# Taking TensorE's closing wait out of a kernel for a batch of expert layers

## The chip, the core and the metric

The kernel runs on one core of one Trainium2 chip. A core has five engines, each with its own list of instructions: TensorE (PE in the profile, with the loading of weights shown apart as PEld), VectorE (DVE), ScalarE (ACT), GpSimd (POOL) and SyncE (SP). The engines order themselves by semaphores: an instruction can raise one, and another can wait until it has reached a value. Transfers between the chip's memory and the core's own memory (DMAs) are issued by SP and POOL here, run by themselves, and raise a semaphore by 16 when they have landed.

The metric is the time of one execution on the device, in microseconds (us). The profile shows a span: from the first instruction of the program to the end of its last one. The time is a little longer than the span.

## The reference

Eight experts, each a two-layer network with a ReLU between the layers, applied to 256 rows of its own:

```python
# x: (8, 256, 512), w1: (8, 512, 2048), w2: (8, 2048, 512), float32
def reference(x, w1, w2):
    h = np.matmul(x, w1)
    h = np.maximum(h, 0)
    return np.matmul(h, w2).astype(np.float32)
```

## The kernel before

All work is in bfloat16 with sums in float32. The list of every engine is written by hand, and each engine runs its own in order; nothing is rearranged by a scheduler. What orders the engines against each other are the semaphores alone.

**Loads.** SP issues the first half of x (`x_f`, line 90). POOL issues the second half (`x_c`, line 140) and all the weights: for each expert one transfer of w1 (line 130) and one of w2 (line 135; the last w2 in two, lines 137 and 138). The weights have room for two experts, so that POOL waits before each later load until PE has used what lay there.

**Computation.** ACT and DVE put x into bfloat16 (line 175), PE turns it round by 64 transposes (line 243), and ACT and DVE copy the result to `xe` (lines 191 and 194). Then PE runs a loop over pairs of experts. For each of the two it computes the first layer (line 259), ACT and DVE apply the ReLU (lines 207 and 224), and then, again for each of the two, PE computes the second layer into `pt_o` (line 281). The last two matmuls of each second layer raise `s_o`, by which ACT (line 211, and for the last two experts line 214) and DVE (line 228, last two experts alone) copy `pt_o` to `out_sb`.

**Stores.** `out_sb` goes out in three transfers, each with its own semaphore of the list `s_out`:

- `s_out[0]`: experts 0 to 3, 2048 KB, issued by POOL (line 164);
- `s_out[1]`: experts 4 to 6, 1536 KB, issued by SP (line 124) when expert 6 is copied;
- `s_out[2]`: expert 7, 512 KB, issued by SP (line 126) when expert 7 is copied.

**The end.** The lists of ACT, DVE and POOL end with their last copy or store (POOL's with a drain of its own work). The function ends with these lines, which belong to two engines:

```python
    pe.wait_ge(s_out[1], 16)

    for s in s_out:
        sp.wait_ge(s, 16)
```

The first is line 290, the last instruction of PE's list. The other is line 293: SP waits for all three stores. As built, SP has two waiting instructions there, one for `s_out[1]`, and after it one for `s_out[2]` and `s_out[0]` together.

Of the kernel before, what the change touches and what calls it, by code (L numbers as in the profile page):

```python
# [9 lines left out]
def kernel(  # L10
# [55 lines left out]
    s_out = [sem(f"s_out{i}") for i in range(3)]  # L66
# [15 lines left out]
    sp, pool, act, dve, pe = nc.sync, nc.gpsimd, nc.scalar, nc.vector, nc.tensor  # L82
# [163 lines left out]
    with pe.Fori(0, G) as g:  # L246
# [21 lines left out]
        with pe.Fori(0, 2) as b:  # L268
            for kt in range(KT2):
# [10 lines left out]
                for m in range(MT):  # L280
# [6 lines left out]
                    )  # L287
                    if kt == KT2 - 1:
                        ins.then_inc(s_o, 1)
    pe.wait_ge(s_out[1], 16)  # L290

    for s in s_out:
        sp.wait_ge(s, 16)
# [30 lines left out]
```

## Time and profile before

| what | value |
|---|---|
| time, median of 3 runs | 181.29 us (181.14 to 182.26) |
| time of the profiled execution | 180.94 us |
| its span | 179.2 us |
| PE busy | 128.7 us, 72% |
| PEld busy | 88.3 us, 49% |
| ACT busy | 54.1 us, 30% |
| DVE busy | 40.9 us, 23% |
| POOL busy | 13.8 us, 8% |
| share of the 16 DMA engines' time taken by the software queue (POOL's) | 93.7% |
| the same by the hardware queue (SP's) | 6.0% |
| mean granted TensorE clock | 0.989 |

An engine's busy time counts its computing instructions. Waits on semaphores, branches and the issuing of transfers are not in it. The profile can still list a wait as an instruction of the line that made it: an entry `PEldq` or `SPq` is such an instruction of PE's or SP's queue, and its duration is that of the instruction once its condition holds, not the time spent waiting. For a transfer the profile gives the time from its issue to its landing.

### The profile page before, as it was taken

Reading aid. Unit: us, or ns where it says so; the run is one execution under the profiler, and the core shown is the slowest. Engines: PE = TensorE matmul, PEld = TensorE weight load, DVE = VectorE, ACT = ScalarE, POOL = GpSimd, SP = SyncE. Lnnn points to the kernel's source line nnn. Section 1 sums busy time; section 2 is a strip of 40 time slices with the busy share of each in tenths; the row PEclk is TensorE's granted clock in tenths of the full one; section 3 lists DMA queues with packets and bytes.
Section 4 is the critical chain, followed back from the end, with each engine's and each line's share of the span. In section 5 each row is a group of like instructions: output and inputs, shape, how many; then the busy total and the mean of one; then the engine's idle time right before and its main releaser. Section 6 shows DMA issues by size and latency. Waiting matters only on the chain. (4 is left out here: it accounts for less than half of the span.)

```text
span 179.2 us, 2548 instructions
## 1 busy us (share of the span) xinstructions
PE 128.7 (72%) x824; PEld 88.3 (49%) x832; DVE 40.9 (23%) x42; ACT 54.1 (30%) x49; POOL 13.8 (8%) x25
## 2 busy tenths in 40 slices
PE   0040403099799979979997998989589596989890
PEld 0030303078687434868742487874134485854330
DVE  0725527262333000333300033330000132310100
ACT  2759596952222020422202033130200231220100
POOL 3910000000101010110101010000100400000000
PEclk9999999999999999999999999999969999999999
DMA  5999999989989999999998999999999899999997
GB/s 192 340 225 234 212 198 234 227 187 230 227 187 230 227 198 219 234 216 194 234 223 190 230 227 198 219 234 216 194 234 223 190 230 227 198 210 216 305 420 302
DMA packets 4240, 40.90 MB, mean 228 GB/s; under 512 B 400, under 2 KB 400, under 8 KB 2064
## 3 DMA queue, kind: packets, MB, share of 16 engines
q0 software_dynamic: 3120, 36.70, 93.7%
q1 hardware_dynamic: 1120, 4.19, 6.0%
HBM read 71.30 MB, written 4.19 MB: 421 GB/s over the span
## 5 line engine op out<-in xcount | busy, mean ns | idle before, releaser
L259 PE MATMUL pt_h<-xe,w_sb 128*128 x512 | 64.0, 280 | 7.8 <-PEq L85 6.9
L259 PEld LDWEIGHTS pt_h<-xe,w_sb 128*128 x512 | 56.9, 146 | 15.3 <-issue 14.1
L281 PE MATMUL pt_o<-w_sb,ht_sb 128*128 x248 | 57.8, 387 | 7.7 <-PEq L85 6.1
L224 DVE TENSOR_SCALAR ht_sb<-pt_h 128x512 bf16<-128x512 f32 x32 | 22.1, 692 | 97.0 <-PE pt_h L259 97.0
L281 PEld LDWEIGHTS pt_o<-w_sb,ht_sb 128*128 x256 | 24.9, 99 | 39.4 <-issue 13.1
L207 ACT ACTIVATE ht_sb<-pt_h 128x512 bf16<-128x512 f32 x32 | 19.1, 597 | 49.1 <-PE pt_h L259 49.1
L243 PE MATMUL pt_tr<-identity,x_b 128*128 128x128 bf16 x64 | 7.5, 309 | 30.2 <-PEq L85 30.2
L243 PEld LDWEIGHTS pt_tr<-identity,x_b 128*128 128x128 bf16 x64 | 6.5, 142 | 30.9 <-issue 30.9
L211 ACT COPY out_sb<-pt_o 128x1024 f32<-128x1024 f32 x6 | 6.1, 1017 | 44.7 <-PE pt_o L281 44.7
L175 ACT CAST x_b<-x_f 128x1024 bf16<-128x1024 f32 x2 | 10.3, 5174 | 1.5 <-DMA x_f<-in_x_dram 1.5
L130 POOL DMA_DIRECT2D w_sb<-in_w_dram x8 | 4.2, 533 | 77.7 <-PE pt_h L259 77.7
L175 ACT COPY x_b<-x_c 128x1024 bf16<-128x1024 bf16 x2 | 9.6, 4778 | 0.0
L135 POOL DMA_DIRECT2D w_sb<-in_w_dram x7 | 6.4, 913 | 35.6 <-PE pt_o L281 35.5
L175 DVE CAST x_b<-x_f 128x1024 bf16<-128x1024 f32 x2 | 6.1, 3058 | 5.6 <-DMA x_f<-in_x_dram 5.6
L194 DVE COPY xe<-pt_tr 128x1024 bf16<-128x1024 bf16 x2 | 4.9, 2460 | 8.5 <-PE pt_tr L243 8.5
L194 ACT COPY xe<-pt_tr 128x1024 bf16<-128x1024 bf16 x2 | 5.0, 2483 | 4.1 <-PE pt_tr L243 4.1
L214 ACT COPY out_sb<-pt_o 128x512 f32<-128x512 f32 x2 | 1.2, 585 | 14.6 <-PE pt_o L281 14.6
L175 DVE COPY x_b<-x_c 128x1024 bf16<-128x1024 bf16 x2 | 5.4, 2680 | 0.0
L228 DVE COPY out_sb<-pt_o 128x512 f32<-128x512 f32 x2 | 1.4, 692 | 15.0 <-PE pt_o L281 15.0
L191 ACT COPY xe<-pt_tr 128x1024 bf16<-128x1024 bf16 x2 | 2.0, 1012 | 4.1 <-PE pt_tr L243 4.1
L191 DVE COPY xe<-pt_tr 128x1024 bf16<-128x1024 bf16 x2 | 1.4, 691 | 7.8 <-PE pt_tr L243 7.8
L175 ACT ACT_TABLE_LOAD x1 | 1.3, 1283 | 2.9 <-PEq L96 2.9
(10 smaller groups left out, 3.4 us busy)
## 6 DMA issues: line engine op xcount, KB each, us to landing
w_sb<-in_w_dram POOLq DMA_DIRECT2D x15, 2048.0 KB, 24.9
x_f<-in_x_dram SPq DMA_DIRECT2D x4, 512.0 KB, 4.6
out_dram<-out_sb POOLq DMA_DIRECT2D x1, 2048.0 KB, 34.5
out_dram<-out_sb SPq DMA_DIRECT2D x1, 1536.0 KB, 8.6
w_sb<-in_w_dram POOLq DMA_DIRECT2D x1, 1152.0 KB, 25.3
x_c<-in_x_dram POOLq DMA_DIRECT2D x1, 1024.0 KB, 10.7
w_sb<-in_w_dram POOLq DMA_DIRECT2D x1, 896.0 KB, 29.0
out_dram<-out_sb SPq DMA_DIRECT2D x1, 512.0 KB, 4.0
```

The lines of the kernel that those rows point to most:

```text
L130: pool.dma_start(w1_k[:, e % 2 * KT1:(e % 2 + 1) * KT1], w1_r[e]).then_inc(s_w1[e], 16)
L135: pool.dma_start(w2_k[:, k:k + KT2], w2_r[e]).then_inc(s_w2[e], 16)
L175: copy(x_b[:, b].rearrange("p (t m) q -> p m q t", m=MT), src.rearrange("p m (q t) -> p m q t", t=KT1),).then_inc(t_xb, 1)
L191: copy(xe[:, a * n:(a + 1) * n], pt[b][:].rearrange("p j q -> p (j q)")).then_inc(s_xe[b], 1)
L194: copy(xl[:, :, :, :, a - G].rearrange("p l j q -> p j l q"), pt[b][:].rearrange("p j (l q) -> p j l q", l=G),).then_inc(s_xe[b], 1)
L207: act.activation(ht[:, k:k + FB // 2, :C], ph[1][:], relu).then_inc(t_ha, 1)
L211: act.copy(o_sb[:, e + b], po[:]).then_inc(s_act, 1)
L224: dve.tensor_relu(ht[:, k:k + FB // 2, :C], ph[0][:]).then_inc(t_hb, 1)
L228: dve.tensor_copy(o_sb[:, e + b, 0], po[:, 0]).then_inc(s_dve, 1)
L243: ins = pe.transpose(pt[b][:, j], x_b[:, b, j], identity[:])
L259: ins = pe.matmul(ph[i // 2][:, i % 2, :], ws[i % 2 * KT1 + kt], xs[kt], start=(kt == 0), stop=(kt == KT1 - 1),)
L281: ins = pe.matmul(po[:, m], hs[(kt - k0) * MT + m], ws[kt - k0], start=(kt == 0), stop=(kt == KT2 - 1),)
```

## The change

The wait at the end of PE's list is deleted. PE's list then ends with the loop over pairs of experts, as ACT's and DVE's end with their last copies. The waits of SP stay.

```diff
@@ -287,7 +287,6 @@
                     )
                     if kt == KT2 - 1:
                         ins.then_inc(s_o, 1)
-    pe.wait_ge(s_out[1], 16)
 
     for s in s_out:
         sp.wait_ge(s, 16)
```

The built programs differ in that one instruction: every other instruction stands on the same engine, in the same order, with the same waits.

## The prediction

> **What bounds the kernel now.** I read the views from the outside in: first the page for the span, then the window table over the last part, then the order of instructions there, and last the waits that end the program. The page's stores and the clock come first.
>
> ```profile
> span 179.2 us, 2548 instructions
> PEclk9999999999999999999999999999969999999999
> DMA  5999999989989999999998999999999899999997
> out_dram<-out_sb POOLq DMA_DIRECT2D x1, 2048.0 KB, 34.5
> out_dram<-out_sb SPq DMA_DIRECT2D x1, 1536.0 KB, 8.6
> out_dram<-out_sb SPq DMA_DIRECT2D x1, 512.0 KB, 4.0
> ```
>
> The row DMA is near 9 in almost every one of the 40 slices: through its body the kernel is bound by transfers. The change touches nothing in that body, so what it is worth has to be read at the very end. There, three stores remain, and the last column says how long each takes from its issue to its landing. The timeline of the end, in order of start, says when the work before them is over (columns: start, duration, engine, line, what, and the idle time before):
>
> ```profile
> 167.37 7.07 PE L281 MATMUL pt_o<-w_sb,ht_sb 128*128 x31 [0.79 <-PEq L85]
> 169.25 0.40 SPq L124 DMA_DIRECT2D out_dram<-out_sb  x1
> 174.26 0.69 DVE L228 COPY out_sb<-pt_o 128x512 f32<-128x512 f32 x1 [7.17 <-PE pt_o L281]
> 174.47 0.58 ACT L214 COPY out_sb<-pt_o 128x512 f32<-128x512 f32 x1 [7.27 <-PE pt_o L281]
> 175.09 0.35 SPq L126 DMA_DIRECT2D out_dram<-out_sb  x1
> ```
>
> The matmuls end at 167.37 + 7.07 = 174.44 us. ACT's copy ends at 174.47 + 0.58 = 175.05, and SP issues the last store at 175.09. From there no engine computes any more. The stores land, by these starts and the times to landing above, at 169.25 + 8.6 = 177.85 (`s_out[1]`) and at 175.09 + 4.0 = 179.09 (`s_out[2]`). POOL's store, `s_out[0]`, needs one row more, that of its line:
>
> ```profile
> L164 POOL DMA_DIRECT2D out_dram<-out_sb x1: 763/763/763, 140.6 to 140.6; - x1
> ```
>
> 140.6 + 34.5 = 175.1. So the three land in the order `s_out[0]`, `s_out[1]`, `s_out[2]`, with about 1.2 us between the last two. Then the waits themselves, PE's at line 290 and SP's at line 293 (duration least/median/most in ns, then the first and last start), and SP's time spent waiting there (total, times, longest):
>
> ```profile
> L290 PEldq EVENT_SEMAPHORE  x1: 51/51/51, 177.9 to 177.9; - x1
> L293 SPq EVENT_SEMAPHORE  x2: 17/22/28, 177.9 to 179.2; - x2
> SPq L293 <- DMA out_dram<-out_sb: 3.7, 2, 2.4
> ```
>
> PE's wait and SP's first one pass together at 177.9, when `s_out[1]` lands. SP's second passes at 179.2, where the span ends. Of SP's 3.7 us there, 2.4 go to the first wait and 3.7 - 2.4 = 1.3 to the second. **What ends the program is SP's wait for the last store; PE's wait is over 1.3 us earlier.**
>
> **The change part by part.** There is one part: PE's wait goes. It removes one instruction of 51 ns, which passes at 177.9. What it moves is the moment at which PE has nothing left in its list: from 177.9 + 0.05 = 177.95 to the end of its matmuls, 174.44, which is 3.5 us earlier. It adds nothing, and no transfer, loop or load is moved past another: the lists are otherwise the same.
>
> Three questions decide the sum. *Who waits for PE?* Behind the removed instruction PE has nothing queued in this program, and nobody else waits for what PE would do after its matmuls; the last thing that others take from PE is `pt_o`, at 174.26 and 174.47 in the timeline. So inside the span the gain is 0. *What is late next?* The wait was never the latest; SP's second wait at 179.2 stays, and it depends on a store issued at 175.09, which depends on ACT and DVE, not on PE's ending. *What lies outside the span?* The profiled execution took 180.94 us, so 180.94 - 179.2 = 1.74 us lie around the span, in which the core closes the execution; no view shows who does what in it. This is the only place where an earlier PE could count.
>
> I bound that unknown from both sides. On the one side, all 1.74 us could be PE's own closing work, begun only when its list is done: then it would now begin 3.5 us earlier, and the end could fall at most to SP's 179.2, a gain of 1.74 us. On the other side, PE's closing could cost something where it now lies. A meeting of the engines is shown at the start of the program, and two rows of the waits give its price to the engine that comes early:
>
> ```profile
> SPq L308 <- PEq L308: 0.7, 1, 0.7
> POOL x_c L140 <- POOLq L96: 2.9, 1, 2.9
> ```
>
> In the first, SP waits 0.7 us for PE until all engines have met; the second is the 2.9 us that POOL spends on all that stands ahead of its first transfer, SP's first loads and several meetings among it. I take 0.7 as the price of one meeting more and keep 2.9 as the far end, which would need a whole opening to be repeated. What value do I take? By the first of these rows the one who comes early waits and the last to come lets all go. If the close has such a meeting too, the last to come is SP at 179.2, before the change and after it, and PE only waits longer. The value is therefore 0, from the row nearest to the situation; the range keeps a part of both ends.
>
> [...]
>
> A second price concerns the clock of TensorE. The window table shows it where PE has finished (columns: window, length, busy time and count of PE, PEld, DVE, ACT, POOL, granted clock, share of the DMA engines, GB/s):
>
> ```profile
> 174.45:177.90 3.45, 0.00 (x0) 0.00 (x0) 0.50 (x1) 0.58 (x1) 0.00 (x0) 1.00 1.00 412
> 177.90:179.20 1.30, 0.00 (x0) 0.00 (x0) 0.00 (x0) 0.00 (x0) 0.00 (x0) 0.86 0.06 22
> ```
>
> PE computes nothing in either window. The granted clock is 1.00 in the first and 0.86 on average in the second, although PE stood in its wait through the first window. So the wait does not keep the clock up: it falls within the last 1.3 us, while PE has been idle since 174.44. If the close ran slower at a lower clock, that would be paid already. I take 0 for this too, and what it would cost if the wait did hold the clock is at most that the 1.74 us take twice as long.
>
> [...]
>
> **The sum** is 0 in the span and 0 around it: 180.94 us for an execution such as the profiled one. The median of the three runs, 181.29, is 0.35 us above it, and I forecast against that median: 181.3 us.
>
> **The rivals.**
>
> *PE's closing is on the path (faster).* If PE's own close, begun at 177.95, is what ends at 180.94, it takes 2.99 us; begun at 174.44 it would be over at 177.43, before SP's last wait, and the end would be set by what SP needs after 179.2. For it speaks only that PE's wait passes as late as 177.9, close enough to the end that 3 us of work would reach it. Against it speaks that SP passes its own wait 1.3 us after PE, so that PE's close would have to be over 1.3 us longer than SP's to matter. The greatest gain is 1.74 us, to 179.55 by the median; half of it, 0.87 us, gives 180.4. That the largest gain is 1.74 / 180.94 = 0.96% leaves almost nothing for faster by over 1%.
>
> *PE's closing meets the last stores (slower).* In the window from 174.45 to 177.90 the DMA engines are full (share 1.00, 412 GB/s): the rest of `s_out[1]` and most of the last store go through there. Before, PE ended behind this stretch; after, it ends at its beginning. If PE's ending moves bytes of its own (instructions that are fetched, or records that are written), they now stand in line ahead of packets of the last store, and SP's second wait is later by their length. The price: one of 16 engines moves 412 / 16 = 25.75 GB/s, so 8 KB on the one that finishes last cost 0.32 us, and 16 KB 0.64 us. It decides from the first byte on that engine, since nothing hides behind the last store; for 1% (1.8 us) 46 KB on one engine would be needed. Against it speaks the second window: from 177.90 on the DMA share is 0.06, though PE's ending lies in it now, so whatever PE moves there is small. I price it at 16 KB: 181.29 + 0.64 = 181.9; with one meeting (0.7) instead, 182.0, which is the same to what can be told.
>
> *The change doesn't do what it says.* PE could be held at its end anyway, by something at the close that waits until all are done. Then the wait only stood in front of another wait, and the time is the forecast's, 181.3. The trace cannot tell this from the forecast, and I count it there.
>
> **How the numbers follow.** The forecast, with the third case in it, has a chance of 0.82 at 181.3; its own scatter is that of the three runs, 181.14 to 182.26, with most of it near the lower end. The slower rival has 0.13, at 181.9 with a tail towards 183 (the doubled 1.74 us) and beyond; the faster rival 0.05, at 180.4. A measurement of this kernel can tell about 1% from no change, that is 1.8 us. Over 1% slower, above 183.1, lies the far end of the slower rival and what I cannot name: 0.07. Over 1% faster, below 179.5, lies beyond the largest gain: 0.02. Within 1%: 0.91. The range runs from 180.8, half a microsecond under the median and so beyond the lowest run shown, to 182.1, which takes in the slower rival at 181.9 and 182.0.
>
> **What would show it.** In the profile after: line 281's last matmul ends near 174.4 and the last store is issued near 175.1; the entry of line 290 is gone; SP's two waits, one line higher, pass near 177.9 and 179.2; the span is 179.2 within 0.3 us, and the time lies 1.7 us above it. If the closing of PE were on the path, the span would stay and the 1.74 us around it would shrink. If it met the stores, the last store's 4.0 us to landing would grow, and with it the span. The prediction is wrong if the 1.74 us grow without a change in the span, since I have no mechanism for that, or if anything ahead of 174 us moves, since no instruction there differs.

## The result, and the profile after

Without the wait the kernel took 180.75 us as the median of 20 executions (180.23 to 181.63), beside 181.63 us for the kernel before in as many (180.12 to 182.67). The ratio is 0.9962, with a 95% interval of 0.9944 to 0.9981: about 0.4% faster, within the 1% that I had called no change, but with an interval that leaves out 1, and not the 0 of my sum. The time lies 0.05 us under the range that I gave, 180.8 to 182.1.

The profile after shows an ending as before. From its page, the span and the stores (the last column is us from issue to landing):

```profile
span 178.8 us, 2547 instructions
...
out_dram<-out_sb POOLq DMA_DIRECT2D x1, 2048.0 KB, 36.7
out_dram<-out_sb SPq DMA_DIRECT2D x1, 1536.0 KB, 8.6
...
out_dram<-out_sb SPq DMA_DIRECT2D x1, 512.0 KB, 4.5
```

The timeline of its end (start, duration, engine, line, what, and the idle time before):

```profile
166.52 7.07 PE L281 MATMUL pt_o<-w_sb,ht_sb 128*128 x31 [0.79 <-PEq L85]
...
168.83 0.40 SPq L124 DMA_DIRECT2D out_dram<-out_sb  x1
173.41 0.69 DVE L228 COPY out_sb<-pt_o 128x512 f32<-128x512 f32 x1 [7.16 <-PE pt_o L281]
173.62 0.59 ACT L214 COPY out_sb<-pt_o 128x512 f32<-128x512 f32 x1 [7.27 <-PE pt_o L281]
174.23 0.35 SPq L126 DMA_DIRECT2D out_dram<-out_sb  x1
```

And SP's closing waits, now line 292 (duration least/median/most in ns, first and last start):

```profile
L292 SPq EVENT_SEMAPHORE  x2: 17/22/28, 177.5 to 178.7; - x2
```

There is one instruction less, all of the end lies 0.4 to 0.9 us earlier than in the profile before, and the chain is the same: matmuls, copies, last store, SP's last wait. This shift of the span is not the gain. The spans spread over 178.6 to 180.0 us after, and over 178.3 to 180.1 before; the mean is 179.13 us over 31 executions after (the 20 above and those of the second experiment) and 179.04 over 143 executions before (those that ran beside the experiments, on four chips). Of each kernel one execution, over 1.5% above the fastest, is left out of these figures and of those below.

What differs is the time around the span. In those same executions, time minus span was:

| kernel | executions | short | long | mean |
|---|---|---|---|---|
| before | 143 | 15, of 1.70 to 1.80 us | 128, of 2.42 to 3.17 us | 2.67 us |
| after | 31 | 29, of 1.60 to 1.69 us | 2, of 2.71 and 2.82 us | 1.71 us |

So what lies around the span is about 1 us shorter in most executions. I call it the close, since what differs will show up behind the program. The execution of before that was profiled, 180.94 - 179.2 = 1.74 us, was one of the rare short ones.

### The profile page after: what moved, and what is told of

It reads as the page before. It is cut to its first block, busy times and chain, and to the rows that moved or that the text cites. A ratio compares the mean times of both kernels' runs of the same rounds, so it can differ in the third digit from the quotient of the medians.

```text
span 178.8 us, 2547 instructions
## 1 busy us (share of the span) xinstructions
PE 126.0 (70%) x824; PEld 87.1 (49%) x832; DVE 40.9 (23%) x42; ACT 54.1 (30%) x49; POOL 14.3 (8%) x25
## 5 line engine op out<-in xcount | busy, mean ns | idle before, releaser
L259 PE MATMUL pt_h<-xe,w_sb 128*128 x512 | 62.9, 277 | 9.6 <-PEq L85 8.7
L259 PEld LDWEIGHTS pt_h<-xe,w_sb 128*128 x512 | 56.2, 146 | 16.8 <-issue 16.1
L281 PE MATMUL pt_o<-w_sb,ht_sb 128*128 x248 | 56.1, 379 | 7.9 <-PEq L85 6.2
L281 PEld LDWEIGHTS pt_o<-w_sb,ht_sb 128*128 x256 | 24.4, 97 | 38.3 <-issue 11.2
L130 POOL DMA_DIRECT2D w_sb<-in_w_dram x8 | 4.3, 535 | 76.3 <-PE pt_h L259 76.3
L135 POOL DMA_DIRECT2D w_sb<-in_w_dram x7 | 3.7, 533 | 35.7 <-PE pt_o L281 35.7
L145 POOL TENSOR_SCALAR_AFFINE_SELECT identity<-identity 128x128 bf16<-128x128 bf16 x1 | 3.5, 3491 | 0.2 <-POOL identity L143 0.2
```

The lines of the kernel that those rows point to most:

```text
L130: pool.dma_start(w1_k[:, e % 2 * KT1:(e % 2 + 1) * KT1], w1_r[e]).then_inc(s_w1[e], 16)
L135: pool.dma_start(w2_k[:, k:k + KT2], w2_r[e]).then_inc(s_w2[e], 16)
L145: pool.affine_select(out=identity[:], in_=identity[:], compare_op=mybir.AluOpType.not_equal, fill=1.0, base=0, pattern=[[-1, P]], channel_ ...
L259: ins = pe.matmul(ph[i // 2][:, i % 2, :], ws[i % 2 * KT1 + kt], xs[kt], start=(kt == 0), stop=(kt == KT1 - 1),)
L281: ins = pe.matmul(po[:, m], hs[(kt - k0) * MT + m], ws[kt - k0], start=(kt == 0), stop=(kt == KT2 - 1),)
```

## The experiments

I began with three theories. CLOSE: the close is longer because PE reaches its end late. SCATTER: the difference comes from the spans of the executions, not from the change. PLACE: not the waiting counts but the instruction, since it moves by one place all that the core runs behind PE's list. Three more names come up in the expectations. ENDING: what counts is that PE's list ends with a semaphore instruction behind its loops. KIND: only a waiting instruction at the end does it. LOOPS: the place of PE's main loops decides. Diffs are against the kernel after unless said otherwise, shortened to the lines that matter, with remarks of mine behind `#`; `s_pad` is a further semaphore that nobody reads, and the line that makes it is left out. "Around" means time minus span; three numbers are its least, median and most over 8 to 12 executions. Where an instruction is only added, the kernel computes what the one after computes.

### The two kernels again

The kernel before with an empty line more:

```diff
     pe.wait_ge(s_out[1], 16)
+
```

> The kernel of before with an empty line more, to see the span of each execution beside its time. Theory CLOSE (what lies around the span grows when PE reaches its end late): time minus span is about 1.74 us in most executions and some 1.2 us more, near 2.9, in a part of them; the ratio to before is 1.000. Theory SCATTER (the 0.4% comes from spans that differ from execution to execution, not from the change): time minus span is 1.74 us in all executions, and the spans spread over 178.4 to 181 us.

> The kernel after, once more, on the same chip as the others of this call. CLOSE: time minus span about 1.64 us in nearly all executions, ratio 0.994 to 0.998. SCATTER: a ratio whose interval holds 1.000, spans like those of the kernel before within 0.2 us.

Before: 1.73, 2.68, 2.93 us around, ratio 1.0003 (0.9983 to 1.0023). After, with no edit: 1.62, 1.64, 2.71 us, ratio 0.9966 (0.9942 to 0.9990). The result stands, and it lies around the span; SCATTER falls. CLOSE had expected the short kind in most executions of before; it came in 3 of 12. Time minus span of before is of two kinds, and the profiled execution of this run is of the long kind: 181.12 us of time, 178.6 of span. Its windows behind the span show what the first profile could not (window, length, busy times, clock, share of the DMA engines, GB/s):

```profile
178.58:180.42 1.84, 0.00 (x0) 0.00 (x0) 0.00 (x0) 0.00 (x0) 0.00 (x0) 0.50 0.00 0
180.42:181.40 0.98, 0.00 (x0) 0.00 (x0) 0.00 (x0) 0.00 (x0) 0.00 (x0) 0.52 0.06 17
```

The queues of this execution from 178.6 us on (packets, MB, share):

```profile
DMA packets 1, 0.02 MB, mean 6 GB/s; under 512 B 0, under 2 KB 0, under 8 KB 0
## 3 DMA queue, kind: packets, MB, share of 16 engines
q8 instruction: 1, 0.02, 2.0%
```

For 1.84 us nothing moves, and then one packet of a queue of the kind that the profile calls `instruction`: 17 GB/s over 0.98 us are some 16 KB. I call it the fetch below. In the first profile of before, of the short kind, the same stretch is empty:

```profile
179.18:181.40 2.22, 0.00 (x0) 0.00 (x0) 0.00 (x0) 0.00 (x0) 0.00 (x0) 0.55 0.00 0
```

So it is in the profile of the kernel after, of the short kind as well:

```profile
178.75:180.42 1.67, 0.00 (x0) 0.00 (x0) 0.00 (x0) 0.00 (x0) 0.00 (x0) 0.50 0.00 0
180.42:181.40 0.98, 0.00 (x0) 0.00 (x0) 0.00 (x0) 0.00 (x0) 0.00 (x0) 0.88 0.00 0
```

One program, before, thus has a close of 1.74 us without the fetch and of 181.12 - 178.6 = 2.5 us with it.

### A wait that passes at once, and a wait for the last store

```diff
+    pe.wait_ge(s_id, 2)
```

> PE still ends with one waiting instruction, but on a semaphore that has long had its value (the identity matrix, set at about 6 us), so that it passes at once. CLOSE, by the time at which PE ends: as the kernel after, 1.64 us around the span, ratio 0.996. Rival PLACE (the instruction's presence in PE's list counts, not its waiting): as the kernel before, 1.74 us and the long executions, ratio 1.000. SCATTER: ratio 1.000 within its interval.

```diff
+    pe.wait_ge(s_out[2], 16)
```

> PE waits for the store that lands last, s_out[2], instead of s_out[1], so that it ends together with SP, 1.3 us later than before. CLOSE: time minus span grows over 1.74 us in every execution, by 0.3 us or more, and the ratio is over 1.002. PLACE and SCATTER: 1.74 us and ratio 1.000. My prediction's view, that the engine which comes last sets the end: between 0 and 0.2 us more.

The passed wait: 1.71, 2.67, 3.15 us around, ratio 1.0013 (0.9992 to 1.0035), the same as before. PE's last instruction ran at 170.8 us, long ahead of SP's end at 179.3 (the entry of its line):

```profile
L290 PEldq EVENT_SEMAPHORE  x1: 51/51/51, 170.8 to 170.8; - x1
```

The wait for the last store: 2.87, 3.11, 3.36 us, ratio 1.0026 (1.0003 to 1.0049). PE's wait and SP's last one pass together:

```profile
L290 PEldq EVENT_SEMAPHORE  x1: 51/51/51, 179.9 to 179.9; - x1
```

Moving PE's end from 177.9 to 170.8 gains nothing, moving it to 179.9 costs 0.3 to 0.4 us beyond the long kind. This second run came out as CLOSE had expected, and not as PLACE or my prediction had (at most 0.2 us more): PE's end counts once it comes last. In its profile the packet of the instruction queue begins at 182.2 us, 2.2 us behind the span's end instead of 1.84. For the wait that was taken out, CLOSE falls, and PLACE stands.

### One instruction, two, sixteen, sixty-four

```diff
+    pe.sem_inc(s_pad, 1)          # behind the loops
```

> The kernel after, with one instruction at the end of PE's list that raises an unread semaphore and waits for nothing. PLACE (what counts is where the instructions behind the program stand): as before, and as with the passed wait, 2.4 to 3.1 us around the span in most executions, ratio about 1.000. Rival KIND (a waiting instruction at the end does it, another does not): as the kernel after or below it, 1.5 to 1.7 us, ratio 0.992 to 0.997.

2.47, 2.64, 2.93 us around, ratio 1.0002 (0.9980 to 1.0023). An instruction that waits for nothing costs what the wait cost: KIND falls. In its profile the fetch begins 1.8 us behind the span's end, as in that of before.

```diff
+    for _ in range(2):            # 16 and 64 in the other two
+        pe.sem_inc(s_pad, 1)      # behind the loops
```

> The kernel after, with two instructions that raise an unread semaphore at the end of PE's list. PLACE, if a limit lies just behind the list's old length: like before, 2.4 to 3.1 us, ratio about 1.000. If each instruction moved the close by the same amount (0.1 us for the first), 0.2 us more than after and otherwise as after. ENDING: as before.

> The same with sixteen. PLACE with one limit: like before, 2.4 to 3.1 us in most executions, ratio about 1.000, no more than with one or two. PLACE with finer limits: another value, between 1.6 and 3.5 us, in another share of the executions. ENDING: as before.

> The kernel after, with 64 instructions at the end of PE's list that raise an unread semaphore. They run while the last stores are under way, so that the span stays as it is. PLACE: some value between 1.4 and 3.2 us, the same in most executions; as the kernel after (1.62 to 1.69) if the pattern repeats by 64 places. KIND: 1.5 to 1.7 us.

Two: 2.03, 2.26, 2.60 us, ratio 0.9979 (0.9956 to 1.0002). Sixteen: 1.53, 1.56, 1.61 us, ratio 0.9970 (0.9950 to 0.9991). Neither an equal price for each instruction nor one limit beyond which all is slow fits this, and ENDING, by which both would be as before, falls; a place that moves can give it. With sixteen the fetch is inside the span, and the 1536 KB store takes 9.2 us instead of 8.6 (the queues and the issues of its profile):

```profile
q1 hardware_dynamic: 1120, 4.19, 6.0%
q8 instruction: 1, 0.02, 0.0%
...
out_dram<-out_sb SPq DMA_DIRECT2D x1, 1536.0 KB, 9.2
```

The mean span is 179.71 us, against 179.06 of before in the executions beside it: of the 1.3 us gained behind the span by the medians of these (2.84 to 1.56), 0.65 go back inside. Sixty-four miss what I expected: they end the span themselves. They take (179.9 - 170.0) / 63 = 0.157 us each:

```profile
L292 PEldq EVENT_SEMAPHORE  x64: 51/51/51, 170.0 to 179.9; - x64
```

Its 1.77, 1.83, 1.86 us and ratio of 1.0060 (1.0035 to 1.0084) are therefore no clean test. Its fetch, too, lies in the span, at 174.7 us.

### The same numbers at the start of the list

```diff
+    pe.sem_inc(s_pad, 1)          # two, three, four in the others
     pe.wait_ge(s_id, 2)
     with pe.Fori(0, G) as _r:
```

> The kernel after, with one instruction more at the start of PE's list (it raises a semaphore that nobody reads); PE ends without any wait. Theory PLACE (PE's list is one instruction longer, so that what the core runs behind it stands one place later): like the kernel before: time minus span 2.4 to 3.1 us in most executions, ratio about 1.000. Rival ENDING (what counts is that the list ends with a semaphore instruction behind the loop): like the kernel after: 1.62 to 1.69 us in most executions, ratio about 0.996.

> The kernel after, with two instructions at the start of PE's list. PLACE, if only the number of instructions ahead of the close counts: as two at the end, 2.0 to 2.6 us. If the places of PE's loops count as well: another value than with two at the end. KIND: 1.5 to 1.7 us.

> The kernel after, with three instructions at the start of PE's list. LOOPS, by odd and even places: as with one at the start, 1.4 to 1.6 us. LOOPS without such a rule: a value of its own, between 1.4 and 3.1 us.

> The kernel after, with four instructions at the start of PE's list. LOOPS, by odd and even places: as with two at the start, 1.9 to 2.6 us, or as the kernel after, 1.6 to 1.7. LOOPS without such a rule: a value of its own, between 1.4 and 3.1 us.

One: 1.46, 1.50, 1.54 us, ratio 0.9921 (0.9894 to 0.9949), lower than the kernel after (1.64 us, 0.9966), and against PLACE as I had put it: the close stands at the same place as with one at the end. Two: 1.93, 2.09, 2.62 us, ratio 0.9988 (0.9961 to 1.0014), nearly as two at the end. Three: 1.42, 1.47, 1.51 us, ratio 0.9972 (0.9946 to 0.9998); four: 1.46, 1.49, 1.52 us, ratio 0.9962 (0.9946 to 0.9978), which is not as with two, so that a rule of odd and even places falls. With two, the fetch stands behind the span as in the long kind, but sooner, 1.28 us behind its end instead of 1.84:

```profile
179.15:180.43 1.28, 0.00 (x0) 0.00 (x0) 0.00 (x0) 0.00 (x0) 0.00 (x0) 0.50 0.00 0
180.43:181.37 0.94, 0.00 (x0) 0.00 (x0) 0.00 (x0) 0.00 (x0) 0.00 (x0) 0.50 0.06 17
```

With three (and with four) it lies among the stores. The queues of the profile with three, from 174 to 178 us:

```profile
q1 hardware_dynamic: 414, 1.58, 96.7%
q8 instruction: 1, 0.02, 1.5%
```

With one at the start there is none, neither in the span nor behind it:

```profile
179.24:181.20 1.96, 0.00 (x0) 0.00 (x0) 0.00 (x0) 0.00 (x0) 0.00 (x0) 0.55 0.00 0
```

### Which place decides

```diff
+    pe.sem_inc(s_pad, 1)
     with pe.Fori(0, G) as g:      # the main loops
```

> The kernel after, with one instruction more on PE between the loop of the transposes and the main loops. LOOPS (where the main loops stand decides what the close costs): as with one at the start, 1.4 to 1.55 us around the span, ratio about 0.992. BEHIND (only how much stands behind the transposes or in all counts): as with one at the end, 2.4 to 3.1 us, ratio about 1.000.

```diff
     pe.wait_ge(s_id, 2)
+    pe.sem_inc(s_pad, 1)
     with pe.Fori(0, G) as _r:     # the transposes
```

> The kernel after, with one instruction more on PE behind its wait for the identity matrix and ahead of the loop of the transposes. If it is the move of that loop that shortens the close: as with one at the start, 1.4 to 1.55 us around the span. If the total of 133 lengthens it, and the one at the start was short for a reason of its own: 2.4 to 3.1 us.

Between the loops: 2.62, 2.95, 3.10 us, ratio 1.0027 (0.9999 to 1.0055), as at the end; the place of the main loops does not shorten the close, and LOOPS falls. Ahead of the transposes, behind the wait: 1.46, 1.50, 1.55 us, ratio 0.9909 (0.9884 to 0.9934), as at the start. The last three add instructions in both places (one and PE's old wait, one and two, two and one):

```diff
+    pe.sem_inc(s_pad, 1)          # at the start
...
+    pe.wait_ge(s_out[1], 16)      # at the end
```

> The kernel before, PE's wait for s_out[1] in its place, with one instruction more at the start of PE's list. PLACE: not as before, since everything behind stands one place later; near the kernel with two instructions at the end, 2.0 to 2.6 us. KIND: as before, 2.4 to 3.1 us, ratio about 1.000. A third reading (an instruction at the start shortens the close by 0.15 us whatever stands at the end): 0.15 us under before.

```diff
+    pe.sem_inc(s_pad, 1)          # at the start
...
+    for _ in range(2):
+        pe.sem_inc(s_pad, 1)      # at the end
```

> The kernel after, with one instruction at the start of PE's list and two at the end. LOOPS alone: as with one at the start, 1.4 to 1.55 us, ratio about 0.992. If the place of the close counts as well: as with two at the end, 2.0 to 2.6 us, or between the two.

```diff
+    for _ in range(2):
+        pe.sem_inc(s_pad, 1)      # at the start
...
+    pe.sem_inc(s_pad, 1)          # at the end
```

> The kernel after, with two instructions at the start of PE's list and one at the end, 135 in all. If the total decides: as with three at the start, and with one at the start and two at the end, 1.4 to 1.55 us. If the place of the loops decides: as with two at the start, 1.9 to 2.6 us, or more.

The old wait with one at the start: 1.42, 1.46, 1.51 us, ratio 0.9951 (0.9930 to 0.9971). The wait that was taken out costs nothing there, and none of the three expectations for this run held. One and two: 1.43, 1.46, 1.49 us, ratio 0.9934 (0.9909 to 0.9959). Two and one: 1.43, 1.48, 1.50 us, ratio 0.9967 (0.9938 to 0.9997).

The last two are the best pair to see what the fetch does inside the span: 135 instructions each, and the last store issued at nearly the same time (on two chips, though). First two and one, its last issue, then its queues and last store:

```profile
174.39 0.35 SPq L127 DMA_DIRECT2D out_dram<-out_sb  x1
```

```profile
q1 hardware_dynamic: 1120, 4.19, 6.0%
q8 instruction: 1, 0.02, 0.0%
...
out_dram<-out_sb SPq DMA_DIRECT2D x1, 512.0 KB, 5.4
```

Then one and two:

```profile
174.43 0.35 SPq L127 DMA_DIRECT2D out_dram<-out_sb  x1
```

```profile
q1 hardware_dynamic: 1120, 4.19, 5.9%
...
out_dram<-out_sb SPq DMA_DIRECT2D x1, 512.0 KB, 4.1
```

The close is as short in both; but where the queue of instructions moved its one packet, the store needed 5.4 us instead of 4.1, and the span ended at 179.8 instead of 178.6. This pair shows the largest difference: the same store took 4.8 us with three at the start and 4.6 with four, where the fetch lies among the stores too, and 3.6 to 4.6 us in the profiles that have none there. The mean spans are the safer measure: of two kernels with 135 instructions that ran beside each other, three at the start took 179.63 us and one and two 179.04.

That the fetch delays the end, and does not merely stand near it, is borne out by its distance to the end. With two and one, three, and four its packet begins at 176.76, 176.61 and 176.88 us, and the span ends 3.06, 3.09 and 3.07 us later. From the issue of the last store to that end, the same three profiles have 5.4, 4.9 and 4.7 us. (With sixteen, where the store of 1536 KB is the one that takes longer, the distance is 4.0 us.)

### Another engine's list

```diff
+    act.sem_inc(s_pad, 1)         # at the end of ACT's list, PE's as after
```

> The kernel after, with one instruction more at the end of ACT's list, PE's as after. If only the length of PE's list matters (PLACE): as the kernel after, 1.62 to 1.69 us in most executions, ratio about 0.996. If any engine's longer list does it: 2.4 us and more, ratio about 1.000.

1.47, 1.88, 1.97 us around, ratio 0.9966 (0.9935 to 0.9998): between the two expectations, 0.24 us over the kernel after by the medians. From 179.01 us on, behind its span, a packet of about half the size (150 GB/s in one slice of 0.055 us, some 8 KB) stands in another queue:

```profile
q14 instruction: 1, 0.01, 1.3%
```

The queue q8 has no packet in this profile, and in no other profile does q14 have one behind the span.

### Taken together

PE's instructions are counted here as its list has them when it is built, with what stands in a loop counted once.

| PE's instructions (added: start + end) | around, median us | the fetch in the profiled execution |
|---|---|---|
| 132 (the kernel after) | 1.64 | none, in two profiles |
| 133 (0+1: before, the passed wait, one that raises) | 2.64 to 2.68 | 1.8 us behind the span's end |
| 133 (one between the loops) | 2.95 | 1.9 us behind it |
| 133 (0+1: the wait for the last store) | 3.11 | 2.2 us behind it |
| 134 (0+2; 2+0) | 2.26; 2.09 | 1.3 us behind it |
| 135, 136 (3+0, 2+1, 4+0), 148 (0+16) | 1.47 to 1.56 | in the span, among the stores |
| 196 (0+64, which end the span themselves) | 1.83 | in the span, among the stores |
| 133 to 135 (1+0, 1+1, 1+2) | 1.46 to 1.50 | none |

(The kernel before has shown both kinds; its long one stands here.) Where there is a fetch, it comes the sooner the longer PE's list is: 1.8 to 2.2 us behind the span's end with 133 instructions, 1.3 us behind it with 134, and with 135 to 148 among the stores, 3.1 to 4.0 us ahead of it, where it goes with a longer span instead. It is not free: it goes with 0.8 us more of close between the two profiled executions of before (1.74 and 2.5 us), and with 1.3 us more for the last store in the pair above.

What is shown is that the long close and this fetch go together, in the profiles of these kernels and within one of them, and that the number and the place of PE's instructions move both. That the packet carries the instructions which PE runs at the close is argued: q8 had a packet behind or among the stores only where PE's list was lengthened, and q14 behind the span only where ACT's was, but the profile names a queue and no engine. That the fetch is what makes the close long is argued as well. It begins 1.84 us behind the span's end, when a close of the short kind (1.70 to 1.80 us) is already over, so that the long close is late before a byte of it moves; whether the core waits for the fetch from then on, or both have a cause that no view shows, is open.

Three more things stay open. With exactly one instruction ahead of the first loop no profile has a fetch, with none, one or two at the end (1.46 to 1.50 us around the span), and I found no reason; so it is not the place of the close alone that decides. Counted from the span's start, the long executions end 0.7 to 0.9 us after the fetch begins, and so ahead of the end of its packet (181.12 us beside a packet in the window to 181.40); the stall is thus not simply the packet's length. And the kernel before was of the short kind in 1 execution of 10 (the one of these that was profiled had no fetch), with 0.1 us more around the span than the kernel after; neither is explained.

## Why the prediction was right or wrong

**The span: right.** That PE's wait ends nothing, that SP's wait for the last store does, and that the span would not change has held: 179.04 and 179.13 us on the mean. The "within 0.3 us" for two single profiles was too narrow: they differ by 0.4, in a scatter of over 1 us between executions. For the same reason one of the signs that I had set was worth nothing. Something ahead of 174 us did move: the last matmuls end 0.85 us sooner in the profile after. But in the second profile of before, with nothing changed, they end at 173.65 us, 0.79 us sooner than in the first.

**"It adds nothing, and no transfer, loop or load is moved past another": here the prediction failed.** I counted the removed instruction by its 51 ns and by its waiting, and forgot that it occupies a place in PE's list. Without it the close was short in most executions, and neither profile of it has the fetch that goes with the long one: time minus span fell from 2.67 to 1.71 us on the mean, where my sum had 0 around the span. The passed wait and the instruction that raises a semaphore, with closes as long as before, show that its presence cost this, and not its waiting. They do not show that its presence is enough: with one instruction ahead of the first loop, the same wait at the end costs nothing. Why a list of 133 has the fetch, and not where one of them stands ahead of that loop, is open.

That the forecast of 181.3 us still lay within 0.55 us of the result is partly luck: the median of three executions that it rested on was 0.34 us under that of the twenty.

**"1.74 us lie around the span": a number from one execution.** It was the short kind, 15 of 143; the long kind has 2.42 us and more, so that my bound on what could be gained was too low as well. The median of the three runs, 0.35 us above the profiled execution, may have been a sign of it, but their spans are not on record, and the spans scatter by more. A window behind the span of a long execution shows the fetch directly; I read windows only up to the span's end, and took the share of 0.06 in the last of them for a sign that PE's ending moves little.

**"The last to come lets all go": half right.** It makes no difference whether PE ends at 170.8 or at 177.9 (2.67 and 2.68 us around the span). It does once PE comes last: ending with SP at 179.9 costs 0.3 to 0.4 us. I had also placed PE's end at 174.44, the end of its matmuls; PE gets to the end of its list at 170.8 already, while its matmuls still run.

**The clock: no cost shows.** In the profile after it fell sooner behind PE's last matmuls than in that of before, as these windows up to and behind the landing of `s_out[1]` show (0.84 and 0.50, where before had 1.00 and 0.86), and the close was no longer for it (1.67 us, beside the 1.74 of before):

```profile
173.59:177.49 3.90, 0.00 (x0) 0.00 (x0) 0.51 (x1) 0.59 (x1) 0.00 (x0) 0.84 1.03 421
177.49:178.75 1.26, 0.00 (x0) 0.00 (x0) 0.00 (x0) 0.00 (x0) 0.00 (x0) 0.50 0.42 169
```

It need not be the missing wait by which it fell sooner: with the wait in its place and one instruction at the start, the granted clock is 0.83 in the 3.45 us behind the last matmuls. That a lower clock could at most double the close was my estimate; the lowest granted clock in these windows is 0.50, right behind the span in both profiles (179.18 to 180.20 us before, 178.75 to 180.42 after), and the close of both was of the short kind.

**The faster rival: the right sign, the wrong mechanism.** It had PE's close begin earlier, priced at 0.87 us. The gain is 0.69 us by the ratio (0.0038 x 181.63), but an earlier begin has no part in it. The sign that I had set for it, a span that stays and a shorter time around it, came true all the same; only the passed wait told the two mechanisms apart. **The slower rival: a true mechanism in the wrong kernel.** A packet of the instruction queue among the last store's does go with a later end; I priced 16 KB at 0.64 us, and the longer lists with a fetch there, of 135 to 148 instructions, had mean spans 0.5 to 0.8 us above those of before beside them (1.3 us for the store between the two profiles of the pair). But the profile after has no such fetch; it is the kernel before that had one, behind the stores.

## What to carry to other kernels

Here an instruction that waits for nothing cost 1.0 us by its presence at the end of PE's list (2.64 us around the span, beside 1.64). In another kernel, look for packets of the instruction queue in the span and in a window behind it, and try one instruction more and one less on that engine. Compare time minus span over many executions, since a single profile may show the rare kind, as the first one of before did (1.74 us, a kind that came in 15 of 143). One idle instruction at the start of PE's list gave the lowest ratios of all, 0.9921 and 0.9909 in its two forms, against 0.9962 for the change itself. Around the span that is 0.14 us less than the kernel after; the rest of the difference lies in the executions of before beside them, whose closes and spans scatter, and is no gain of its own that these runs show.

## What the hardware showed that I had not expected

A packet of some 16 KB in an instruction queue, 1.3 to 2.2 us behind the span or among the last stores, at the end of most programs here whose PE list has 133 instructions and more; among the stores it goes with 0.5 to 0.8 us more of mean span. The same in another queue, with about half the size and 0.24 us around the span, where ACT's list is one longer. And PE's list was read some 3.6 us ahead of its matmuls: the passed wait, behind the last loop, ran at 170.8 us in a profile whose last copy of PE's result began at 174.41.
